# Layer 1's routing on one Trainium2 core: slots of the first token tile behind its own choice, experts of both tiles behind the slots, seven feature tiles of the rows' product at once

## The chip, the cores and the metric

The kernel runs on one core of one Trainium2 chip. The core has a matrix engine (PE in the profile; PEld is its weight load, which overlaps), a vector engine (DVE), a scalar engine (ACT), GpSimd (POOL) and SyncE (SP, which only issues transfers here), each with an instruction stream of its own that is worked off in order; they wait for each other through semaphores. Sixteen DMA engines move data between HBM and the on-chip memory. The metric is the time of one execution on the device in microseconds (us), as the median of several runs.

## The reference, cut to what matters

Two layers run over 256 latent tokens and 256 context tokens, 1024 features wide. Each layer has three mixers, a product with `w_out`, and a mixture of 16 experts, in 4 groups of 4, of which each token uses the best two of its best group. The last layer (called layer 1, counted from 0) returns latent tokens only.

```python
x_mid = x + mod_x[2] * merge_branches(px[10], y_ret, y_conv, y_mla, w_out)
h2x = rms_norm(x_mid, norm2) * (1.0 + mod_x[4]) + mod_x[3]
# moe(h2x):
scores = jax.nn.sigmoid((t @ w_router).astype(jnp.float32))
biased = scores + router_bias
grp = biased.reshape(-1, 4, 4)
group_score = jnp.sum(lax.top_k(grp, 2)[0], axis=-1)
g_sel = jnp.argmax(group_score, axis=-1)
in_grp = jnp.take_along_axis(grp, g_sel[:, None, None], axis=1)[:, 0]
idx = g_sel[:, None] * 4 + lax.top_k(in_grp, 2)[1]
w = jnp.take_along_axis(scores, idx, axis=1)
w = w / jnp.sum(w, axis=-1, keepdims=True)
for e in range(16):
    he = (jax.nn.silu(t @ w1[e]) * (t @ w3[e])) @ w2[e]
    out = out + gate[:, e:e + 1] * he
```

## The kernel before, in words

Both kernels are written as one long instruction sequence per engine. The program's own scheduler fixes those sequences before the chip starts; nothing is reordered on the chip. `with queued(ins)` and `tc.issue_after(ins)` put instructions behind a named one in that order.

The 256 latent tokens are two token tiles of 128, t=0 and t=1 (`NTT` is 2). Layer 1 comes to its experts in these steps.

- The product with `w_out` is done in two halves of 512 columns; `update` (L1138 to L1142) adds each half to the residual `resid` after a multiplication by a modulation row. The weights come as pieces of 128x1024 that are split into a high part (ACT) and a low part `wlo` (DVE, L383), and PE uses the low part last.
- `features` (L1180 to L1191) transposes `resid` and squares it, `logits_part` and `logits` (L1193 to L1206) make the 16 router scores of a tile in `lt`, `select` (L1216) the biased scores `bi`. In it `group()` finds the best group (`og`, L1240), six steps that each need the one before; `experts()` the two best experts of every group (`o1`, `o2`), eleven such steps; `finish()` keeps those of the chosen group (`sel`). In layer 1 the steps of `experts()` of t=0 run in the gaps of the next tile's work; those of t=1 are put in the list `chosen` and run during the routing.
- `norm2_rows` (L1144) makes the expert inputs `h2` (a product with a modulation row, L1147, and a second instruction, L1149) and, for t=0, its high and low part `h2h` and `h2l` (`hi_lo`, L225 and L226).
- The routing of layer 1 (L1846 to L1890): `positions` (two small matmuls, L1365 and L1366, and `posm`, L1369) numbers the tokens within their group; a comparison with a row of numbers makes the one-hot matrix `ohr` (4 instructions for each tile, L1853), whose rows are tokens and whose columns are 4 groups of 128 slots. The rows' product (L1875) multiplies `h2h` and `h2l` with it. It gathers the tokens by slots: 8 feature tiles, each four matmuls into one PSUM bank, done as two groups of four feature tiles. Each is split into `xgh` (ACT) and `xgl` (DVE) by `hi_lo`.
- `token_gates` and `gates` (L1399 to L1407, L1536 to L1538) make the weight table `gt` of tokens by experts; `slot_gates` (L1880) gathers it by slots with 16 small passes (L1885) into `gsl` (L1887).
- The 16 experts then run in order. Each has three products (`p1`, `p3`, both from `up`, and `down`), each of four weight pieces of 512 KB. For every piece ACT casts the high part `ehi` (L1093), DVE subtracts for the low part `elo` (L1095) and PE does six matmuls (L192, L193, L195). There are four buffers each for `ehi` and `elo`. `act` (L1430 to L1435) makes the activation `eth` in three instructions (tanh on ACT, two on DVE), of which the last needs the gates in `gsl`; `turn_g` transposes it (L1444) and splits it into the two parts of `gg` (L1452 and L1453), with which `down` runs. For expert 0 a function `first` holds the gate work (`slot_gates`, `act`, `turn_g`); it is called between the pieces of expert 1's `p1`, since expert 0's `down` comes after that.

Weight pieces are loaded far ahead by SP into rotating buffers (`offer`, `prefetch`); one of these, in layer 1, has the tag "mr21", which later holds a modulation row, and `fn` (the final norm's row) takes the tag of `ohr`.

## Time and profile before

| | us |
|---|---|
| median of 3 runs | 1630.13 |
| the runs | 1622.14, 1630.13, 1632.17 |
| the profiled execution | 1623.87 (span 1622.1) |
| PE busy, of the span | 1532.8 (94%) |
| DVE busy | 1161.8 (72%) |
| ACT busy | 847.0 (52%) |

The span is the time of the profiled execution from its first to its last instruction; all times of rows are counted from its start. Busy time is what an engine spent in instructions of its own. The granted clock (PEclk) is the share of PE's full speed that it was allowed in a stretch: 1.00 is 2.4 GHz, 0.50 is 1.2 GHz, and a value between is a stretch that had both.

### The profile page before, as it was taken

The numbers are of one execution on the slowest core, as the hardware profiler recorded it, in microseconds if no ns is written. First come the engines' busy times: TensorE is split into PE (matmuls) and PEld (weight loads), VectorE is DVE, ScalarE is ACT, GpSimd is POOL, SyncE is SP. The second block draws the span as 40 slices with busy tenths as digits, with TensorE's granted clock in tenths as the row PEclk, the third lists the DMA queues.
The fourth block names the chain that finished last, engine by engine and source line by source line (L and its number), as shares of the span: only waits on it lengthen the run. The fifth ranks groups of instructions, "written<-read, shape, count | busy, mean of one in ns | idle before, by whom it ended". The sixth has DMA issues, their size and how long they took to land. (4 is left out here: it accounts for less than half of the span.)

```text
span 1622.1 us, 21790 instructions
## 1 busy us (share of the span) xinstructions
PE 1532.8 (94%) x7811; PEld 1191.1 (73%) x7811; DVE 1161.8 (72%) x1978; ACT 847.0 (52%) x1218; POOL 84.8 (5%) x137
## 2 busy tenths in 40 slices
PE   4999999999999997999999969999999989999996
PEld 1766776667767884777777759888978868888775
DVE  3633376426674457899999989577676699999897
ACT  3512233334442223688788845346454467777674
POOL 1011010000000004200000210000000000000000
PEclk8999999999999998999999979999999989999998
DMA  9676354643117448999999956335436579999981
GB/s 343 190 237 227 98 169 139 192 130 105 40 53 257 164 173 300 336 376 364 377 384 373 370 172 182 104 105 150 132 90 208 180 263 371 347 390 326 361 304 64
DMA packets 238281, 370.94 MB, mean 229 GB/s; under 512 B 16147, under 2 KB 133365, under 8 KB 233045
## 3 DMA queue, kind: packets, MB, share of 16 engines
q1 hardware_dynamic: 228944, 345.06, 62.7%
q0 software_dynamic: 6400, 15.13, 3.2%
q10 hardware_dynamic: 2820, 9.28, 1.5%
q8 instruction: 64, 1.05, 0.3%
q14 instruction: 53, 0.43, 0.1%
HBM read 357.69 MB, written 11.73 MB: 228 GB/s over the span
## 5 line engine op out<-in xcount | busy, mean ns | idle before, releaser
L1095 DVE TENSOR_TENSOR elo<-eraw,ehi 128x1024 fp32r<-128x1024 f32 x291 | 344.5, 1218 | 10.3 <-ACT ehi L1093 7.9
L1093 ACT CAST ehi<-eraw 128x1024 fp32r<-128x1024 f32 x291 | 301.2, 1050 | 72.8 <-PE ps L193 44.4
L383 DVE TENSOR_TENSOR wlo<-wraw,whi 128x1024 fp32r<-128x1024 f32 (+1 forms) x146 | 176.4, 1210 | 190.0 <-ACT whi L375 187.8
L375 ACT CAST whi<-wraw 128x1024 fp32r<-128x1024 f32 (+1 forms) x146 | 151.2, 1038 | 275.3 <-PE ps L186 181.6
L185 PE MATMUL ps<-hh,whi 128*128 128x512 f32 (+1 forms) x800 | 286.8, 360 | 4.1 <-ACT hh L427 1.8
L186 PE MATMUL ps<-hl,whi 128*128 128x512 f32 (+1 forms) x800 | 276.5, 346 | 0.1
L187 PE MATMUL ps<-hh,wlo 128*128 128x512 f32 (+1 forms) x800 | 274.9, 345 | 0.3 <-DVE wlo L383 0.3
L185 PEld LDWEIGHTS ps<-hh,whi 128*128 128x128 f32 x800 | 151.1, 189 | 41.9 <-issue 16.5
L186 PEld LDWEIGHTS ps<-hl,whi 128*128 128x128 f32 x800 | 151.2, 189 | 27.8 <-issue 9.5
L187 PEld LDWEIGHTS ps<-hh,wlo 128*128 128x128 f32 x800 | 150.8, 189 | 23.3 <-issue 3.6
L192 PE MATMUL ps<-ehi,xh 128*112 128x512 f32 x256 | 104.0, 406 | 3.9 <-ACT xh L225 3.9
L193 PE MATMUL ps<-ehi,xl 128*112 128x512 f32 x256 | 103.5, 404 | 0.7 <-DVE xl L226 0.6
L192 PE MATMUL ps<-ehi,xgh 128*128 128x512 f32 x256 | 102.3, 400 | 0.2 <-ACT ehi L1093 0.2
L193 PE MATMUL ps<-ehi,xgl 128*128 128x512 f32 x256 | 101.3, 396 | 0.0
L192 PE MATMUL py<-ehi,gg 128*112 128x512 f32 (+1 forms) x240 | 93.6, 391 | 1.8 <-PEq L1562 1.6
L193 PE MATMUL py<-ehi,gg 128*112 128x512 f32 (+1 forms) x240 | 93.1, 390 | 0.0
L1095 DVE TENSOR_TENSOR elo<-raws,ehi 128x1024 fp32r<-128x1024 f32 x72 | 86.0, 1218 | 4.9 <-ACT ehi L1093 2.2
L1093 ACT CAST ehi<-raws 128x1024 fp32r<-128x1024 f32 x72 | 74.7, 1050 | 19.7 <-PE ps L193 11.0
L195 PE MATMUL ps<-elo,xgh 128*128 128x512 f32 x256 | 80.8, 396 | 1.2 <-DVE elo L1095 1.1
L195 PE MATMUL ps<-elo,xh 128*112 128x512 f32 x256 | 80.8, 397 | 0.6 <-DVE elo L1095 0.6
L195 PE MATMUL py<-elo,gg 128*112 128x512 f32 (+1 forms) x240 | 74.7, 393 | 1.5 <-DVE elo L1095 1.4
L959 ACT ACTIVATE pe<-ps,mxv 128x512 f32<-128x512 f32 (+1 forms) x48 | 29.6, 617 | 62.1 <-DVE mxv L957 58.4
(473 smaller groups left out, 2762.9 us busy)
## 6 DMA issues: line engine op xcount, KB each, us to landing
eraw<-in_w_dram SPq DMA_DIRECT2D x291, 512.0 KB
wraw<-in_w_in_dram SPq DMA_DIRECT2D x106, 512.0 KB
adaw<-in_w_ada_dram SPq DMA_DIRECT2D x40, 1024.0 KB
raws<-in_w_dram SPq DMA_DIRECT2D x72, 512.0 KB
wraw<-in_w_out_dram SPq DMA_DIRECT2D x16, 512.0 KB
wraw<-in_w_dram SPq DMA_DIRECT2D x15, 512.0 KB
yd<-ys ACTq DMA_DIRECT2D x16, 448.0 KB
eraw<-in_w_ada_dram SPq DMA_DIRECT2D x13, 512.0 KB
```

The source lines that it names most:

```text
L185: TE.matmul(ps, wp[0], xp[0], start=first, stop=False)
L186: TE.matmul(ps, wp[0], xp[1], start=False, stop=False)
L187: return TE.matmul(ps, wp[1], xp[0], start=False, stop=last).ins
L192: TE.matmul(ps, x_[0], w_[0], start=first, stop=False)
L193: TE.matmul(ps, x_[1], w_[0], start=False, stop=False)
L195: ins = TE.matmul(ps, x_[0], w_[1], start=False, stop=last)
L375: his.append(A.copy(hi[:, :kt * n], raw[:, :kt * n]).ins)
L383: return V.tensor_tensor(lo[:, :kt * n], raw[:, :kt * n], hi[:, :kt * n].bitcast(F32), op=ALU.subtract).ins
L959: A.activation(pe[:, :nk], sps[:, :nk], AF.Exp, scale=MLA_SCALE, bias=mxv[:, 1:2], accum_out=mxv[:, 2:3])
L1093: latest["hi"] = A.copy(hi, raw).ins
L1095: latest["lo"] = V.tensor_tensor(lo, raw, hi.bitcast(F32), op=ALU.subtract).ins
```

## The change

- `update` makes, for layer 1, the first product of `h2` in two halves of 512 columns, each behind its half of `resid`; `norm2_rows` leaves it out there.
- `h2h` of t=0 is cast alone; the subtraction for its `h2l` is put behind the scores `lt` of t=1.
- `positions` and the one-hot rows of t=0 (`group_slots(0)`) come directly behind the group choice of t=0. `experts` and `finish` of both tiles go into `chosen` and run behind the one-hot rows of t=1. The sum `cum` isn't made in layer 1.
- The rows' product does seven feature tiles together, in four banks of the pool `ps`, two of `py` and one of `psa`, and the eighth behind them.
- `ohr` takes the tag "mr21"; the weight buffer that had it, and later `fn`, take a new tag "fn".
- `act` names its last instruction; the reading of the overflow flag (through `latest["act"]`) and the scaling of `fn` are put behind it.

```diff
@@ def update
             V.tensor_tensor(resid[:, T, cs], resid[:, T, cs], tmp, op=ALU.add)
+            if l == 1:
+                if t not in h2:
+                    h2[t] = mg.tile([P, D], F32, name=nm("h2"), tag=("xe", "xe2")[t])
+                V.tensor_tensor(h2[t][:, cs], resid[:, T, cs], mrow[4, T // 2][:, cs], op=ALU.mult)
@@ def norm2_rows
-            V.tensor_tensor(hr, resid[:, T, :], mrow[4, T // 2], op=ALU.mult)
+            if l == 0:
+                V.tensor_tensor(hr, resid[:, T, :], mrow[4, T // 2], op=ALU.mult)
...
-                    hi_lo(h2h[:, t, :], h2l[:, t, :], hr)
+                    A.copy(h2h[:, t, :], hr)
@@ def logits
+            if l == 1 and t == 1:
+                with queued(scaled_):
+                    V.tensor_tensor(h2l[:, 0, :], h2[0], h2h[:, 0, :].bitcast(F32), op=ALU.subtract)
             select(t, lt)
@@ new
+            def group_slots(t):
...
+                rest = positions(og[:, ts, :], cumg[:, ts, :], NG, [d[:, ts, :] for d in slots_])
+                for g in range(NG):
+                    ins = V.tensor_scalar(oh[0][:, t, g, :], C("iota"), posm[:, t, g:g + 1], None, op0=ALU.is_equal)
...
@@ def select
             if l == 1:
                 run(group())
+                chosen.extend([experts, finish])
                 if t == 0:
                     V.tensor_copy(cumg[:, 1, :], og[:, 0, :])
-                else:
-                    chosen.extend([experts, finish])
-                    return
-            both = [group(), experts()] if l == 0 else [experts()]
+                    group_slots(0)
+                return
+            both = [group(), experts()]
@@ routing of layer 1
-            with queued(ins.ins):
+            ins = group_slots(1)
...
+            with queued(ins):
                 scored.append(A.copy(h2h[:, 1, :], h2[1]).ins)
                 V.tensor_tensor(h2l[:, 1, :], h2[1], h2h[:, 1, :].bitcast(F32), op=ALU.subtract)
-                run(chosen[0]())
-                chosen[1]()
+                while chosen:
+                    run(chosen.pop(0)())
+                    chosen.pop(0)()
                 for f in kept:
                     f()
                 token_gates()
...
-            for k4 in range(0, KD, 4):
-                xps = [ps_tile() for _ in range(4)]
+            xps = [ps_tile() for _ in range(4)] + [y for y, _ in ytiles()]
+            xps.append(psa.tile([P, 512], F32, name=nm("psa"), tag="psa"))
+            def rows_by_slots(ks):
...
+            rows_by_slots(range(KD - 1))
+            xps.append(ps_tile())
+            rows_by_slots([KD - 1])
@@ def act
-            V.scalar_tensor_tensor(th[:cap, :], th[:cap, :], gate, p3[:cap, :], op0=ALU.mult, op1=ALU.mult)
+            latest["act"] = V.scalar_tensor_tensor(th[:cap, :], th[:cap, :], gate, p3[:cap, :], op0=ALU.mult, op1=ALU.mult).ins
@@ expert loop
-                    fn = et("ohr", [P, D])
+                    fn = et("fn", [P, D])
...
+                    with tc.issue_after(latest["act"]):
+                        V.tensor_scalar(fn, fn, ROW_SCALE, None, op0=ALU.mult)
```

In the instruction streams the change shows at three places. The first is DVE's stream at the end of the first half of `w_out` (t is the product with the modulation row, h the expert input `h2`, wlo a weight piece's low part). Before:

```order
L1141 TENSOR_TENSOR t_2307_11617<-ps_11543,mr_11125 128x512 [waits PE_49]
L1142 TENSOR_TENSOR resid<-resid,t_2307_11617 128x512 [waits DVE_49]
L1141 TENSOR_TENSOR t_2308_11620<-ps_11544,mr_11125 128x512 [waits PE_49]
L1142 TENSOR_TENSOR resid<-resid,t_2308_11620 128x512 [waits DVE_49]
L383 TENSOR_TENSOR wlo_11631<-wraw_11629,whi_11630 128x1024 [waits DMAHW6_49,Activation_49]
L383 TENSOR_TENSOR wlo_11637<-wraw_11635,whi_11636 128x1024 [waits DMAHW7_49,Activation_49]
L383 TENSOR_TENSOR woalt_11509<-wraw_11641,woalt_11509 128x1024 [waits DMAHW0_49,Activation_49]
```

The two low parts stand directly behind the update of `resid`. And in the changed kernel:

```order
L1141 TENSOR_TENSOR t_2310_11620<-ps_11546,mr_11125 128x512 [waits PE_49]
L1142 TENSOR_TENSOR resid<-resid,t_2310_11620 128x512 [waits DVE_49]
L1141 TENSOR_TENSOR t_2312_11625<-ps_11547,mr_11125 128x512 [waits PE_49]
L1146 TENSOR_TENSOR h_2311_11623<-resid,mr_11127 128x512 [waits DVE_49]
L1142 TENSOR_TENSOR resid<-resid,t_2312_11625 128x512 [waits DVE_49]
L383 TENSOR_TENSOR wlo_11638<-wraw_11636,whi_11637 128x1024 [waits DMAHW6_49,Activation_49]
L1146 TENSOR_TENSOR h_2313_11628<-resid,mr_11127 128x512 [waits DVE_49]
L383 TENSOR_TENSOR wlo_11644<-wraw_11642,whi_11643 128x1024 [waits DMAHW7_49,Activation_49]
```

A half of h2's product now stands ahead of each of the next two low parts.

The second is DVE's stream around the gates. Here elo is a low part of a weight piece, gt the weight table, gsl the gates by slots, eth the activations of experts 0 and 1, den and w the sums and weights of `token_gates`. Before, from the fifth low part behind the rows' product to `gsl`:

```order
L1095 TENSOR_TENSOR elo_12057<-eraw_11497,ehi_12056 128x1024 [waits DMAHW1_49,PE_49,Activation_49]
L1536 TENSOR_TENSOR gt_11917<-o_2286_11533,w__2361_11858 128x2x16 [waits DVE_49]
L1537 TENSOR_TENSOR oge_11857<-o_2287_11534,w__2362_11859 128x32 [waits DVE_49]
L1095 TENSOR_TENSOR elo_12069<-eraw_11499,ehi_12068 128x1024 [waits DMAHW2_49,PE_49,Activation_49]
L1538 TENSOR_TENSOR gt_11917<-gt_11917,oge_11857 128x2x16 [waits DVE_49]
L1095 TENSOR_TENSOR elo_12082<-eraw_11501,ehi_12081 128x1024 [waits DMAHW3_49,PE_49,Activation_49]
L1543 TENSOR_TENSOR ov_12103<-og_11537,keep_11861 128x8
L1434 SCALAR_TENSOR_TENSOR eth_12113<-eth_12113,ps_11982 128x512 [waits Activation_49]
L1545 TENSOR_REDUCE cnt_12105<-ov_12103 128x1 [waits DVE_49]
L1890 TENSOR_TENSOR gov_12111<-gt_11917,ov_12103 128x32
L1095 TENSOR_TENSOR elo_12126<-eraw_11503,ehi_12125 128x1024 [waits DMAHW4_49,PE_49,Activation_49]
L1887 COPY gsl_11981<-ps_12093 128x68 [waits PE_49]
```

The changed kernel, the twelve rows up to `gsl`:

```order
L1095 TENSOR_TENSOR elo_12177<-raws_11831,ehi_12176 128x1024 [waits DMAHW1_49,PE_49,Activation_49]
L1433 RECIPROCAL den_11913<-den_11913 128x2 [waits DVE_49]
L1095 TENSOR_TENSOR elo_12188<-raws_11831,ehi_12187 128x1024 [waits DMAHW2_49,PE_49,Activation_49]
L1434 TENSOR_TENSOR w__2358_11852<-w__2358_11852,den_11913 128x2 [waits DVE_49]
L1435 TENSOR_TENSOR w__2359_11853<-w__2359_11853,den_11913 128x2
L1095 TENSOR_TENSOR elo_12199<-raws_11831,ehi_12198 128x1024 [waits DMAHW4_49,PE_49,Activation_49]
L1564 TENSOR_TENSOR gt_11918<-o_2289_11536,w__2358_11852 128x2x16 [waits DVE_49]
L1565 TENSOR_TENSOR oge_11851<-o_2290_11537,w__2359_11853 128x32 [waits DVE_49]
L1462 SCALAR_TENSOR_TENSOR eth_12255<-eth_12255,ps_12081 128x512 [waits Activation_49]
L1566 TENSOR_TENSOR gt_11918<-gt_11918,oge_11851 128x2x16 [waits DVE_49]
L1919 TENSOR_TENSOR gov_12112<-gt_11918,ov_12104 128x32 [waits DVE_49]
L1916 COPY gsl_11982<-ps_12094 128x68 [waits PE_49]
```

Low parts before carry the numbers 12057, 12069 and 12082 here and in the changed kernel 12177 to 12199: the last write of gt (L1538 before, L1566 now) moved from behind the sixth low part after the last xgl to behind the fourteenth, and behind an activation instruction of expert 1 (eth_12255).

The third is PE's stream at the same point. `ps_12080` (before) and `ps_12081` (now) are expert 1's `p1`, `gt x ohr` the gather of the gates, `cst x eth` the four transposes of expert 0's activation, `py` expert 0's `down`. Before, behind the first piece of `p1`:

```order
L195 MATMUL ps_12080<-elo_12082,xgh_11923 128x512 [waits DVE_49]
L195 MATMUL ps_12080<-elo_12082,xgh_11923 128x512
L1885 MATMUL ps_12093<-gt_11917,ohr_11863 128x17 x8
L1547 MATMUL ps_12107<-cst,cnt_12105 1x1 [waits DVE_49]
L192 MATMUL ps_12080<-ehi_12125,xgh_11923 128x512 [waits Activation_49]
L193 MATMUL ps_12080<-ehi_12125,xgl_11924 128x512
```

The gather has three more pieces of `p1` behind it. Before, around the last of these on PE:

```order
L192 MATMUL ps_12080<-ehi_12149,xgh_11923 128x512 [waits Activation_49]
L193 MATMUL ps_12080<-ehi_12149,xgl_11924 128x512
L1444 MATMUL ps_12117<-cst,eth_12113 128x128 [waits DVE_49]
L1444 MATMUL ps_12117<-cst,eth_12113 128x128 x3
L192 MATMUL ps_12080<-ehi_12149,xgh_11923 128x512
L193 MATMUL ps_12080<-ehi_12149,xgl_11924 128x512
L195 MATMUL ps_12080<-elo_12150,xgh_11923 128x512 [waits DVE_49]
L195 MATMUL ps_12080<-elo_12150,xgh_11923 128x512
L192 MATMUL py_12161<-ehi_12163,gg_12122 128x512 [waits Activation_49]
```

The transposes have four matmuls of that piece behind them, then comes `down`. The changed kernel from the last piece of `p1` on PE:

```order
L192 MATMUL ps_12081<-ehi_12150,xgh_11924 128x512
L193 MATMUL ps_12081<-ehi_12150,xgl_11925 128x512
L195 MATMUL ps_12081<-elo_12151,xgh_11924 128x512 [waits DVE_49]
L195 MATMUL ps_12081<-elo_12151,xgh_11924 128x512
L1914 MATMUL ps_12094<-gt_11918,ohr 128x17 [waits DVE_49]
L1914 MATMUL ps_12094<-gt_11918,ohr 128x17 x7
L1575 MATMUL ps_12108<-cst,cnt_12106 1x1
L1472 MATMUL ps_12118<-cst,eth_12114 128x128 [waits DVE_49]
L1472 MATMUL ps_12118<-cst,eth_12114 128x128 x3
L192 MATMUL py_12162<-ehi_12164,gg_12123 128x512 [waits Activation_49]
```

The gather of the gates and the transposes, which stood inside expert 1's `p1` with matmuls of its pieces behind them, now stand in one row behind all of `p1`, directly ahead of `down`.

## Rows read from the trace of the kernel before

**Rows 1.** Stretches: us, busy us and instructions by engine, PEclk, DMA share, GB/s.
```profile
1300.00:1320.00 20.00, 14.20 (x57) 11.40 (x58) 19.42 (x86) 11.98 (x21) 1.24 (x2) 0.74 0.79 262
1320.00:1340.00 20.00, 20.00 (x98) 16.09 (x97) 18.09 (x32) 14.16 (x16) 0.00 (x0) 1.00 0.80 275
1420.00:1520.00 100.00, 100.00 (x444) 80.71 (x443) 95.98 (x98) 76.84 (x83) 0.00 (x0) 1.00 0.98 360
```
**Rows 2.** Groups by line, 1320 to 1520: busy us, mean ns | idle before, releasers.
```profile
L1095 DVE TENSOR_TENSOR elo<-eraw,ehi 128x1024 fp32r<-128x1024 f32 x105 | 124.3, 1217 | 2.0 <-ACT ehi L1093 1.5
```
**Rows 3.** Timeline, halves of w_out: start us, us, engine line ... [idle before <-releaser].
```profile
1282.88 0.69 DVE L1142 TENSOR_TENSOR resid<-resid,t 128x512 f32<-128x512 f32 x1
...
1284.76 0.50 PE L186 MATMUL ps<-wlo,mh 128*128 128x512 f32 x1 [0.57 <-DVE wlo L383]
```
**Rows 4.** Timeline of PE from the end of w_out to the first expert.
```profile
1296.79 0.39 PE L187 MATMUL ps<-woalt,bt 128*128 128x512 f32 x1
...
1307.77 1.19 PE L1875 MATMUL ps<-ohr,h2h 128*128 128x512 f32 x2 [4.15 <-DVE gs L1235]
...
1312.72 1.09 PE L1875 MATMUL ps<-ohr,h2l 128*128 128x512 f32 x4
...
1318.11 0.40 PE L192 MATMUL ps<-ehi,xgh 128*128 128x512 f32 x1
```
**Rows 5.** Timeline of DVE from the one-hot rows of t=1 to the last xgl.
```profile
1309.51 0.88 DVE L1853 TENSOR_SCALAR ohr<-cmoe,posm 128x128 fp32r<-128x128 f32 x4
...
1314.46 0.68 DVE L226 TENSOR_TENSOR xgl<-ps,xgh 128x512 fp32r<-128x512 f32 x1
...
1319.51 0.68 DVE L226 TENSOR_TENSOR xgl<-ps,xgh 128x512 fp32r<-128x512 f32 x1
```
**Rows 6.** Timeline of DVE from the third piece's low part to the gated activation.
```profile
1320.30 1.21 DVE L1095 TENSOR_TENSOR elo<-eraw,ehi 128x1024 fp32r<-128x1024 f32 x1
1321.43 0.17 DVE L1402 TENSOR_REDUCE w__2362_11859<-oge 128x2 f32<-128x32 f32 x1
1321.53 1.21 DVE L1095 TENSOR_TENSOR elo<-eraw,ehi 128x1024 fp32r<-128x1024 f32 x1
...
1327.68 0.18 DVE L1538 TENSOR_TENSOR gt<-gt,oge 128x32 f32<-128x32 f32 x1
...
1328.99 0.67 DVE L1434 SCALAR_TENSOR_TENSOR eth<-eth,ps 128x512 f32<-128x512 f32 x1
1329.59 0.15 DVE L1545 TENSOR_REDUCE cnt<-ov 128x1 f32<-128x8 f32 x1
...
1332.60 0.23 DVE L1887 COPY gsl<-ps 128x68 f32<-128x68 f32 x1 [1.62 <-PE ps L1885]
...
1333.94 0.74 DVE L1435 SCALAR_TENSOR_TENSOR eth<-eth,gsl,ps 128x512 f32<-128x512 f32 x1
```
**Rows 7.** Timeline of PE: gather of the gates, transposes, expert 0's down.
```profile
1330.70 1.86 PE L1885 MATMUL ps<-gt,ohr 128*128 128x17 f32 x16
...
1335.97 0.60 PE L1444 MATMUL ps<-cst,eth 128*128 128x128 f32 x4
...
1337.33 0.67 PE L192 MATMUL py<-ehi,gg 128*128 128x512 f32 x2
```
**Rows 8.** Stretches around two changes of the granted clock; columns as in rows 1.
```profile
1301.00:1302.00 1.00, 0.98 (x8) 0.90 (x7) 0.94 (x7) 0.03 (x1) 0.00 (x0) 0.79 0.97 307
...
1307.80:1311.40 3.60, 3.60 (x10) 2.88 (x11) 3.53 (x11) 1.97 (x4) 0.61 (x1) 0.50 0.73 241
...
1311.00:1312.00 1.00, 1.00 (x4) 0.78 (x3) 1.00 (x5) 1.00 (x3) 0.00 (x0) 0.59 0.90 238
```
**Rows 9.** Timeline of PE: waits at the flag of layer 0 and behind expert 11.
```profile
848.50 0.49 PE L193 MATMUL ps<-ehi,xl 128*112 128x512 f32 x1 [0.63 <-DVE xl L226]
...
1538.07 0.74 PE L195 MATMUL ps<-elo,xgh 128*128 128x512 f32 x2 [0.75 <-DVE elo L1095]
...
1541.54 0.73 PE L195 MATMUL ps<-elo,xgh 128*128 128x512 f32 x2 [0.40 <-DVE elo L1095]
```

More of the change, by code (lines that the diff above doesn't have):

```diff
@@ L1182, in features @@
             cs = slice(half * 512, half * 512 + 512)
-            if half == 0:
+            if half == 0 and l == 0:
                 h2[t] = mg.tile([P, D], F32, name=nm("h2"), tag=("xe", "xe2")[t % 2])
@@ L1359, in row @@
             return C(name).unsqueeze(1).to_broadcast([P, NTT, n])
-        def positions(sel, cum, n, dst):
-            pps = ps_tile()[:, :sel.shape[1] * n]
-            TE.matmul(pps, C("ones"), cum, start=True, stop=False)
-            TE.matmul(pps, C("tri"), sel, start=False, stop=True)
-            flat = "p t e -> p (t e)"
-            posn, keep, posm = (d.rearrange(flat) for d in dst)
-            V.scalar_tensor_tensor(posm, pps, 1.0, sel.rearrange(flat), op0=ALU.add, op1=ALU.mult)
-            def rest():
-                V.scalar_tensor_tensor(keep, pps, float(cap), sel.rearrange(flat), op0=ALU.is_lt, op1=ALU.mult)
-                A.copy(posn, pps)
-            return rest
         if l == 0:
```

49 lines of the change are left out of this document (32 added, 17 removed).

## Prediction

> **What bounds the kernel now.** I read the stretches first, because the average shares of the whole span mix stages. In the expert stage (the last line of [rows 1]) PE is busy 100.00 of 100 us at the full clock, DVE 95.98 of 100: PE sets the pace and DVE follows with 4% to spare. In the routing (1300 to 1320) it is the other way round: PE works 14.20 of 20 us, and at a mean clock of 0.74, while DVE works 19.42. From 1320 to 1340 PE is full again and DVE has 18.09. So time is lost in the routing, by PE waiting for DVE's chain, and behind it every microsecond by which PE starts later or stops stays in the total, as long as nothing else is waited for. Transfers are not: over 200 us the 105 low parts of the weights stood idle for 2.0 us in all, 1.5 of them for ACT's cast and not for a piece [rows 2].
>
> Then the timeline of PE in the routing. The rows' product begins at 1307.77 after 4.15 us of nothing, and the first expert matmul at 1318.11 [rows 4]. DVE's timeline beside it: one-hot rows of t=1 at 1309.51, first `xgl` at 1314.46, eighth at 1319.51 (0.72 each with the small instructions between) [rows 5], third low part at 1320.30 and from there one low part after the other [rows 6].
>
> **The change part by part.** The program order of the changed kernel is known, so I walk it with the prices of these rows. On DVE a low part takes 1.13 until the next can begin (1320.30 to 1321.43), a small instruction 0.10 (1321.43 to 1321.53), a 128x512 activation instruction 0.60 (1328.99 to 1329.59) [rows 6].
>
> *Halves of h2's product, positions of t=0.* A half ahead of the first low part of `w_out` costs some 0.6, by the 0.69 of an instruction of its size [rows 3]; PE already waits 0.57 there for that low part, so `w_out` ends about 0.6 later, and two small passes among its last matmuls add 0.3. In return only a half instead of the whole product stands ahead of t=0's group choice, 0.6 less. I take 0 for the choice of t=0. If the cover were gone, 0.3 would be left.
>
> *`h2l` of t=0 and the one-hot rows.* `h2l` (1.13) moves from ahead of the scores of t=1 to behind them, and the biased scores of t=1 wait for it, since DVE has nothing else in its order. The four one-hot rows of t=0 (0.22 each, a quarter of the 0.88) and its slots come out of t=1's chain. I get t=1's one-hot rows some 0.6 later (1310.1 to 1310.9, bounds −0.6, if DVE used all its 0.58 idle us of 1300 to 1320, and +1.0). Small instructions that are gone from that point give 0.2 back: first `xgl` at 1314.85, eighth done at 1320.6, +0.4.
>
> *Seven feature tiles.* Both parts of t=0 now run while t=1 is still choosing. For t=1 remain 14 matmuls and the eighth tile's four, 0.23 each (four in 1.09, of which the last one's 0.40 overlaps nothing [rows 4]): from `h2l` of t=1 at about 1311 to 1315.2. The first expert matmul can start at 1315.5 instead of 1318.11, −2.6. But the third piece needs its low part, which stands behind all eight `xgl` in DVE's order: done at 1321.9, 0.4 later than before. So PE's lead is spent waiting, in bits, between 1317 and 1323.
>
> *The experts' choice behind the slots.* This is the term that decides. Before, the last write of `gt` stood behind six low parts and began at 1327.68; PE gathered the gates at 1330.70 without a wait and had matmuls of expert 1's `p1` to do until 1337.33 [rows 7], under which copy, activation and transposes lay. Now eleven steps of choosing for t=0 and eleven for t=1, `sel`, and `token_gates` are threaded between low parts, one or two to a gap. Fourteen low parts at 1.13 are 15.8, 24 small instructions 2.4, two activation instructions 1.2: 19.4 from 1320.7, so the last write of `gt` begins at 1340.1. I take off 0.2, because the many that depend on nothing recent are nearer 0.08: done at 1340.1.
> PE's `p1` of expert 1 needs the tenth of these low parts. Nine and its own 1.21, 17 small ones and one activation instruction are 13.6: 1334.3, and two more matmuls end `p1` at 1334.8. In the new order the gather is next on PE, and behind it, in order, the transposes and `down`. PE has nothing to do for 5.3 us.
> From 1340.1: gather 1.86, `gsl` and a cast 0.3, activation 0.74 (its step; 1333.94) [rows 6], transposes 0.60 and from their end 0.76 to `down` (before, 1335.97 + 0.60 to 1337.33 [rows 7]); with 0.1 to 0.2 for handing over, 1344.45. Before, `down` began at 1337.33: **+7.1**. DVE is then four pieces ahead, the most that the buffers allow, and PE is the bound to the end, so this isn't given back. From below: the fourteenth low part can't be earlier than expert 1's `p1` is done with its buffers, which leaves a gap of 3.1 whatever DVE's prices: **+5**.
>
> *The clock.* After gaps of this kind the granted clock falls: dense matmuls ended at 1297.18 [rows 4], and behind small work and pauses the stretch 1301 to 1302 shows 0.79, half way to the lower level of 1.2 GHz; 1307.8 to 1311.4, when PE had begun again, shows 0.50, and only 1311 to 1312 shows 0.59 on its way back [rows 8]. Here PE stands still for 5.3 us, so I expect the gather, and perhaps the first of `down`, at the lower level. The gather is then 1.1 to 1.9 longer, the rest 0 to 1.8: **+2.0**, bounds 0 and +3.7.
> The Trainium skill says the same against this change ("TensorE: Matmul & The Clock Gate", section "HAM oscillation — how this bites in real kernels"): a stall long enough between two bursts brings the array back to the lower clock, and the next burst starts cold. By that rule the gap costs +9.1; without it +7.1.
>
> *Two places further on.* At layer 0's flag PE waits 0.63 for an `xl` that stood behind a low part; now the low part is behind it: −0.5. Behind expert 11, PE waits 0.75 and 0.40 for low parts that stood behind the scaling of `py` [rows 9]; the new order has them ahead: −1.15, bounds 0 and −1.5.
>
> *At nothing:* buffer "fn" and the earlier loads of two rows, hidden as transfers are [rows 2] (uncovered, one piece of 512 KB is 1.5 at 360 GB/s [rows 1]); `cum`, four small instructions in a stretch already counted; the scaling of `fn`, one 0.7 us instruction on DVE with 4% to spare.
>
> **Sum.** 7.1 + 2.0 − 0.5 − 1.15 = +7.45, or +7.5 on the profiled execution's 1623.87: 1631.3. That execution lies 6 under the median of the runs shown, which spread over 10 us. The mean of these four executions is 1627.1, and I take that as the base: 1634.6, rounded to **1635**.
>
> **The rivals.**
> *The gap without the clock.* PE idles, but the clock holds: +7.1 less the 1.65 of the two places, +5.5, 1632.6. For it: from 1297.2 on PE had small work and the fall still took over 4 us, so a 5.3 us gap may just reach it.
> *The gates come in time* (the other side). One mechanism: DVE's small instructions vanish in gaps that it has anyway (1.62 idle at 1332.60 [rows 6]), and the last write of `gt` is done before `p1` of expert 1 ends. Then the earlier start counts: −2.6 − 1.65 = −4.2, 1622.9. It decides if `gt` is written 5.3 earlier than I have it, or if `p1` ends so much later; the buffers' rule (gap of 3.1) speaks against it.
> *The change doesn't do what it says.* The product is earlier, but DVE's eight `xgl` and the low parts set the same times as before, and no gap follows because I count the low parts wrongly: +0.4 − 1.65 = −1.2, 1625.9.
> *The lower clock holds into down.* PE restarts with short passes and transposes, and all four pieces of `down` run at the lower level before it returns: gap +7.1, clock +3.7, less 1.65: +9.2, 1636.3. [...]
> *Late pieces.* The standstill also holds up ACT's casts and the buffers behind them, and PE meets a second gap of its size at expert 1's own gates: +15, 1642.
>
> **Chances.** Forecast 0.43, gap without the clock 0.22, lower clock into `down` 0.10, gates in time 0.10, does nothing 0.08, late pieces 0.07. The likeliest alone: 1629 to 1640. Three runs that spread like these move a median by up to 5, so the range goes from 1624 to 1645: it leaves out the gates in time and some of the late pieces. About 1% is what a measurement of this kernel can tell, 1613.8 and 1646.4: faster 0.03, slower 0.08, within it 0.89.
>
> **What would show it.** In the changed profile: first expert matmul near 1315.5 but no gain at the third piece; an idle of 3 to 6 us in front of the gather, released by the last write of `gt` on DVE; a clock of 0.50 in the gather; `down` of expert 0 seven to eleven later. The waits at 848.50, 1538.07 and 1541.54 gone. It is wrong if the gather starts with no wait, if DVE is idle between 1321 and 1340, or if `down` starts by 1338.

## The result, and the profile after

The changed kernel takes 1639.41 us (median of 9 runs, 1636.16 to 1641.35), the kernel before 1626.52 (median of 9, 1622.14 to 1632.17): a ratio of 1.0072, 95% interval 1.0060 to 1.0084. It is slower by 0.7%. The forecast was 1635, with a range of 1624 to 1645, and "within 1%" at 0.89. The profiled execution has a span of 1639.6.

The stretches of the changed kernel, columns as in [rows 1] (us, busy us and instructions of PE, PEld, DVE, ACT, POOL, granted clock, DMA share, GB/s). They lie some 7 us later than before, because `w_out` ends at 1304.66 and no longer at 1297.18; about half of that is the scatter of executions, below.

```profile
1300.00:1320.00 20.00, 16.19 (x71) 12.86 (x70) 14.55 (x61) 7.07 (x16) 1.20 (x2) 0.74 0.62 204
1320.00:1340.00 20.00, 18.21 (x76) 13.44 (x75) 20.00 (x52) 16.15 (x22) 0.00 (x0) 1.00 0.66 220
1420.00:1520.00 100.00, 99.14 (x439) 79.72 (x438) 96.33 (x99) 75.96 (x81) 0.00 (x0) 1.00 0.94 341
```

Where [rows 1] had PE at 20.00 of 20 and DVE at 18.09, it is now DVE that has no idle time (20.00) and PE that waits for it (18.21). The timeline of PE (start, us, engine, line ... [idle before <-releaser]) shows the rest; it answers to [rows 4, 7]:

```profile
1304.26 0.40 PE L187 MATMUL ps<-woalt,bt 128*128 128x512 f32 x1
...
1319.37 1.17 PE L1900 MATMUL ps<-ohr,h2h 128*128 128x512 f32 x4 [0.60 <-DVE keep L1227]
...
1323.77 0.50 PE L192 MATMUL ps<-ehi,xgh 128*128 128x512 f32 x1
...
1330.08 0.73 PE L195 MATMUL ps<-elo,xgh 128*128 128x512 f32 x2 [1.36 <-DVE elo L1095]
...
1342.69 0.63 PE L195 MATMUL ps<-elo,xgh 128*128 128x512 f32 x2
1348.14 3.60 PE L1914 MATMUL ps<-gt,ohr 128*128 128x17 f32 x16 [4.82 <-DVE gt L1566]
1351.67 0.19 PE L1575 MATMUL ps<-cst,cnt 128*1 128x1 f32 x2
1352.85 1.11 PE L1472 MATMUL ps<-cst,eth 128*128 128x128 f32 x4 [0.99 <-DVE eth L1463]
1354.65 1.22 PE L192 MATMUL py<-ehi,gg 128*128 128x512 f32 x2 [0.69 <-ACT gg L1480]
...
1362.37 0.39 PE L192 MATMUL ps<-ehi,xgh 128*128 128x512 f32 x1
```

PE ends expert 1's `p1` at 1343.32, stands still for 4.82 us until DVE has written `gt`, gathers in 3.60 us (before, 1.86 without a wait [rows 7]), waits 0.99 for the gated activation and 0.69 for its cast, and only then begins `down`, at 1354.65. The 1.36 at 1330.08 is the third piece, whose low part stands behind all eight `xgl`. DVE at the same places, to be laid beside [rows 5, 6]:

```profile
1310.07 0.16 DVE L1224 SCALAR_TENSOR_TENSOR posm<-ps,og 128x4 f32<-128x4 f32 x1 [0.60 <-PE ps L1221]
...
1318.15 0.16 DVE L1224 SCALAR_TENSOR_TENSOR posm<-ps,og 128x4 f32<-128x4 f32 x1 [1.06 <-PE ps L1221]
...
1323.03 0.68 DVE L226 TENSOR_TENSOR xgl<-ps,xgh 128x512 fp32r<-128x512 f32 x1
...
1328.04 0.68 DVE L226 TENSOR_TENSOR xgl<-ps,xgh 128x512 fp32r<-128x512 f32 x1
...
1328.81 1.21 DVE L1095 TENSOR_TENSOR elo<-eraw,ehi 128x1024 fp32r<-128x1024 f32 x1
...
1345.97 1.21 DVE L1095 TENSOR_TENSOR elo<-raws,ehi 128x1024 fp32r<-128x1024 f32 x1
...
1347.91 0.18 DVE L1566 TENSOR_TENSOR gt<-gt,oge 128x32 f32<-128x32 f32 x1
...
1351.78 0.23 DVE L1916 COPY gsl<-ps 128x68 f32<-128x68 f32 x1 [3.47 <-PE ps L1914]
```

The low parts at 1328.81 and 1345.97 are the first and the last of the fourteen that stand between the last `xgl` and `gt`. Last, the clock (windows, columns as above): in the standstill, in the gather, and from the start of `down` to the next expert matmul.

```profile
1345.00:1346.00 1.00, 0.00 (x0) 0.00 (x0) 1.00 (x4) 0.00 (x0) 0.00 (x0) 0.73 1.05 408
1348.14:1351.74 3.60, 3.60 (x18) 3.56 (x18) 0.17 (x1) 0.00 (x0) 0.00 (x0) 0.50 1.01 377
1358.00:1359.00 1.00, 1.00 (x4) 0.80 (x3) 1.00 (x1) 0.00 (x0) 0.00 (x0) 0.50 0.00 0
1359.00:1360.00 1.00, 1.00 (x5) 0.77 (x4) 0.06 (x1) 0.70 (x1) 0.00 (x0) 0.94 0.00 0
1354.65:1362.37 7.72, 7.72 (x24) 6.08 (x25) 3.71 (x4) 3.42 (x4) 0.00 (x0) 0.71 0.24 71
```

PE's last work before the fall ends at 1343.32. The clock falls within 1345 to 1346 (0.73 on average over that microsecond), is at the lower level, 1.2 GHz, through the whole gather, and returns only at about 1359, when `down` is more than half done.

**How two executions are compared.** Executions of the same kernel differ (the kernel before took 1622.14 to 1632.17), and between its two profiles nearly all of the difference arises ahead of about 1272 us: the second (run e5_same) lies 6.77 us behind the first there, and 6.83 at the end. So I set the start of each PE matmul against the same matmul of the kernel before and read two numbers for each kernel: the *tail*, what it gains or loses from the end of layer 1's attention to the end of the span, and the *early part*, summed over the 1036 of the first 1272 us in which the kernels that move no tile repeat to 0.14 us. Times from the end of `w_out`'s last matmul:

| kernel | first expert matmul | `down` of expert 0 begins | next expert matmul | tail | early part |
|---|---|---|---|---|---|
| before | 20.93 | 40.15 | 46.03 | 0 | 0 |
| changed | 19.11 | 49.99 | 57.71 | +10.78 | +2.97 |
| e1_early | 19.19 | 40.81 | 46.68 | +3.46 | +2.90 |
| e2_late | 20.83 | 47.20 | 55.50 | +6.75 | −0.14 |
| e3_fill | 17.84 | 46.87 | 55.06 | +8.12 | +2.96 |
| e4_merged | 17.78 | 39.44 | 45.25 | +1.45 | +1.76 |
| e5_same | 20.90 | 40.13 | 46.00 | +0.06 | −0.09 |
| e6_seven | 20.41 | 40.01 | 45.90 | −0.09 | −0.02 |
| e7_lean | 18.00 | 39.68 | 45.49 | −0.80 | +1.58 |
| e9_nof | 17.74 | 48.63 | 55.90 | +8.59 | +2.8 |
| e11_aligned | 18.07 | 39.73 | 45.63 | +0.03 | +0.01 |
| e12_pool | 19.46 | 41.03 | 46.96 | +1.41 | +0.3 |

How far the tail can be trusted depends on the clock in the routing. With the routing of the kernel before, kernels repeat it to 0.1 us (e5_same +0.06, e8_alloc +0.05). The changed kernel, e3_fill and e9_nof have the same instructions in the same order up to the first expert matmul, and yet it comes at 19.11, 17.84 and 17.74. The windows of the changed kernel, then of e9_nof:
```profile
1308.00:1318.00 10.00, 8.39 (x27) 6.76 (x27) 7.97 (x30) 2.71 (x6) 1.20 (x2) 0.50 0.86 292
```
```profile
1309.60:1316.40 6.80, 4.93 (x13) 3.63 (x13) 6.28 (x29) 1.32 (x3) 0.63 (x1) 0.50 0.98 327
1316.50:1320.00 3.50, 2.81 (x14) 2.06 (x13) 3.07 (x12) 2.98 (x5) 0.57 (x1) 1.00 0.76 201
```
The lower level lasts some 10 us in one and 7 in the other. So a tail behind the changed routing carries up to 1.4 us that is a matter of the execution.

The tail of +10.78 is made up of: `w_out`'s second half +0.7; −1.8 up to the first expert matmul; +11.7 from there to `down`; +1.84 in `down` (7.72 for 5.88); +1.1 and +0.9 for two new waits further on; −2.3 behind expert 11; −1.2 near the end; −0.2 in small pieces. The +3 of the early part lies where no instruction was changed. Together 13.8; the runs measured +11.7 (9.8 to 13.7).

### The profile page after: what moved, and what is told of

Its sections match the earlier page's. It is cut to its first block, busy times and chain, and to the rows that moved or that the text cites. A ratio compares the mean times of both kernels' runs of the same rounds, so it can differ in the third digit from the quotient of the medians.

```text
span 1639.6 us, 21793 instructions
## 1 busy us (share of the span) xinstructions
PE 1545.3 (94%) x7811; PEld 1200.4 (73%) x7811; DVE 1164.4 (71%) x1979; ACT 850.1 (52%) x1218; POOL 84.5 (5%) x137
## 5 line engine op out<-in xcount | busy, mean ns | idle before, releaser
L192 PE MATMUL py<-ehi,gg 128*112 128x512 f32 (+1 forms) x240 | 95.7, 400 | 1.5 <-PEq L1590 0.9
L193 PE MATMUL py<-ehi,gg 128*112 128x512 f32 (+1 forms) x240 | 94.3, 396 | 0.0
```

What stands on the lines that cost most here:

```text
L192: TE.matmul(ps, x_[0], w_[0], start=first, stop=False)
L193: TE.matmul(ps, x_[1], w_[0], start=False, stop=False)
```

## The experiments

Each runs as a whole kernel beside the kernel before. Theory 1 of the expectations is the prediction's: the experts' choice of t=0, behind the slots, makes `gt` late, and PE's stop ahead of the gather, with the clock, is the loss. What the rivals say stands in each expectation.

**e1_early: the changed kernel with the choice of t=0 back where it was.**
```diff
-                chosen.extend([experts, finish])
                 if t == 0:
                     V.tensor_copy(cumg[:, 1, :], og[:, 0, :])
                     group_slots(0)
-                return
-            both = [group(), experts()]
+                else:
+                    chosen.extend([experts, finish])
+                    return
+            both = [group(), experts()] if l == 0 else [experts()]
...
```


> One part of the change undone: the experts of t=0 are chosen where the kernel before chose them, in the gaps of t=1's scores; everything else is the change. The last write of the gate table then stands behind seven low parts instead of fourteen, and PE's gather of the gates stands inside expert 1's p1 again. Theory 1 (the late gate table makes the loss): no wait of PE in front of the gather, expert 0's down 39 to 41 us behind the end of w_out (before 40.2, change 50.0), ratio to the kernel before 0.997 to 1.000. Theory 2 (the slots of t=0 and the seven feature tiles make the loss, by waits in the routing): down still 5 us or more later, ratio 1.004 to 1.008.


Ratio 1.0043 (1.0028 to 1.0057). PE's timeline, third piece and gather:
```profile
1328.28 0.73 PE L195 MATMUL ps<-elo,xgh 128*128 128x512 f32 x2 [1.14 <-DVE elo L1095]
...
1337.00 1.85 PE L1915 MATMUL ps<-gt,ohr 128*128 128x17 f32 x16
```
The gather waits for nothing and runs at full speed, `gt` stands behind seven low parts instead of fourteen, and `down` begins at 40.81 instead of 49.99. So the place of this choice is worth 9.2 us at `down`, as theory 1 has it. But the time should have come back to the kernel before and did not: 3.46 are left in the tail, of which 2.0 are the two new waits further on, and 2.90 in the early part.

**e2_late: the kernel before with this one edit alone.**
```diff
                 run(group())
+                chosen.extend([experts, finish])
                 if t == 0:
...
-                run(chosen[0]())
-                chosen[1]()
+                while chosen:
+                    run(chosen.pop(0)())
+                    chosen.pop(0)()
```


> One part of the change alone on the kernel before: the experts of t=0 are chosen behind the slots, with those of t=1; slots, halves and the product in two groups of four stay as before. The last write of the gate table stands behind fourteen low parts. Theory 1: PE waits 3 to 6 us in front of the gather, which runs at the lower clock; ratio to the kernel before 1.005 to 1.009. Theory 2: nothing is lost, 0.999 to 1.001.


Ratio 1.0042 (1.0029 to 1.0054), a little less than expected; tail +6.75. PE's timeline at the same place:
```profile
1344.88 2.64 PE L1884 MATMUL ps<-gt,ohr 128*128 128x17 f32 x16 [3.86 <-DVE gt L1536]
1348.63 1.11 PE L1442 MATMUL ps<-cst,eth 128*128 128x128 f32 x4 [0.99 <-DVE eth L1433]
1350.43 1.22 PE L192 MATMUL py<-ehi,gg 128*128 128x512 f32 x2 [0.69 <-ACT gg L1450]
```
The edit alone makes the standstill, the slower gather, and the waits of 0.99 and 0.69. It is the largest part of the loss, with the early part at nothing.

**e3_fill: the changed kernel with 18 more matmuls in the standstill**, whose product nobody reads.
```diff
...
+                if e == 1:
+                    spare = psa.tile([P, 512], F32, name=nm("psa"), tag="psa")
+                    with tc.issue_after(latest["mm"]):
+                        for i in range(FILL):
+                            TE.matmul(spare, xh[:, 0, :P], xh[:, i % KD, :], start=(i == 0), stop=(i == FILL - 1))
```


> The changed kernel with 18 matmuls of 128x512 more, whose result nobody uses, on PE between the end of expert 1's p1 and the gather of the gates: 4.2 us of PE work in its wait of 4.8. They take nothing from DVE. If the lower clock costs what the trace of the change shows (gather 3.60 for 1.86, expert 0's down 7.72 for 5.88, some 0.5 in the transposes, 4.1 in all), the clock stays at 1.00, the gather takes 1.9, and the loss falls from 0.72% to 0.4 to 0.5% (ratio 1.004 to 1.005). If the clock costs nothing on the path, the ratio stays at 1.007 or rises.


Ratio 1.0049 (1.0030 to 1.0069). PE's timeline:
```profile
1341.02 4.28 PE L1976 MATMUL psa<-xgh 128*128 128x512 f32 x18
1346.02 1.96 PE L1915 MATMUL ps<-gt,ohr 128*128 128x17 f32 x16 [0.72 <-DVE gt L1567]
...
1349.08 0.90 PE L1473 MATMUL ps<-cst,eth 128*128 128x128 f32 x4 [0.98 <-DVE eth L1464]
1350.66 1.22 PE L193 MATMUL py<-ehi,gg 128*128 128x512 f32 x2 [0.69 <-ACT gg L1481]
```
and the windows of the gather, of a microsecond behind it, and of `down`:
```profile
1346.02:1347.98 1.96, 1.96 (x18) 1.93 (x18) 0.17 (x1) 0.00 (x0) 0.00 (x0) 1.00 1.05 393
1349.00:1350.00 1.00, 0.90 (x4) 0.50 (x4) 0.28 (x2) 0.00 (x0) 0.00 (x0) 0.67 0.88 336
1350.66:1358.85 8.19, 8.19 (x25) 6.46 (x25) 3.71 (x4) 3.41 (x4) 0.00 (x0) 0.66 0.30 104
```
With work in the gap the gather is at the full clock: 1.96 instead of 3.60, so 1.64 of it was the clock's. But the clock did not stay up: it fell in the microsecond from 1349, after waits of 0.72 and 0.98 with only the gather's narrow matmuls between them, and `down` is no faster than without the filling (8.19, against 7.72). The clock's share in the gather is shown by this; that in `down` (+1.84, at 0.71) is read from the rows, and this run did not take it away. Of the 2.66 by which the tail is below the changed kernel's, 1.27 lie ahead of the first expert matmul, where the filling can have no part.

**e4_merged: the changed kernel with the experts of both tiles chosen by the same instructions**, on `[P, 2, 16]` instead of twice on `[P, 16]`: 14 small instructions instead of 28.
```diff
...
-                while chosen:
-                    run(chosen.pop(0)())
-                    chosen.pop(0)()
+                experts2()
```


> The changed kernel, but the experts of both token tiles are chosen by the same 14 instructions over both tiles instead of 28 over one each (the sum of the two choices, which layer 1 does not use, is left out). The last write of the gate table stands behind seven low parts. Theory 1: no wait in front of the gather, expert 0's down 38 to 41 us behind w_out, ratio to the kernel before 0.996 to 1.000. Theory 2: as the change, 1.004 to 1.008.


Ratio 1.0031 (1.0020 to 1.0042), above the expected 0.996 to 1.000; tail +1.45, in which the two new waits further on (0.89 and 0.48 here) stand as in e1_early. PE's gather and DVE's last write of `gt`, a timeline of each:
```profile
1337.80 1.85 PE L1940 MATMUL ps<-gt,ohr 128*128 128x17 f32 x16
```
```profile
1336.53 0.17 DVE L1594 TENSOR_TENSOR gt<-gt,oge 128x32 f32<-128x32 f32 x1
```
Both tiles chosen behind the slots, and yet no wait: `gt` is written 1.1 before PE wants it. What hurt was the number of small dependent instructions, each in a gap of its own between low parts, and not the place as such. `down` begins 0.71 earlier than before, in an execution with the short stretch of the lower clock (e1_early, with the long one, 0.66 later).

**e5_same: the kernel before, again**, to see what two runs of one kernel differ by.

> The kernel before once more, unchanged, as a measure of what two builds of one program differ by, and with a second profile of it. If the 3 to 5 us by which the profiled executions of all variants so far lie behind that of the kernel before at the start of w_out's second half (1272 us) are scatter of executions, this profile lies behind by as much there too, and the ratio is 0.998 to 1.002. If it lies at the same time as the first profile (within 1 us), the variants lose something ahead of the routing that the change makes.


Ratio 0.9993 (0.9981 to 1.0004).

**e6_seven: the kernel before with seven feature tiles at once**, and nothing else.
```diff
-                xps = [ps_tile() for _ in range(4)]
+            xps = [ps_tile() for _ in range(4)] + [y for y, _ in ytiles()]
+            xps.append(psa.tile([P, 512], F32, name=nm("psa"), tag="psa"))
...
```


> One part of the change alone on the kernel before: seven feature tiles of the rows' product at once, the eighth behind them; slots and the experts' choice as before. Theory (DVE sets the pace up to the third weight piece): the first expert matmul comes 1 to 2.6 us earlier behind the end of w_out than the 20.9 of before, expert 0's down less than 1 us earlier than 40.2; ratio 0.999 to 1.001. Rival (PE sets it): down 1.5 to 2.6 us earlier, ratio 0.998.


Ratio 1.0007 (0.9997 to 1.0017). The first expert matmul comes 0.5 earlier, `down` 0.14, the tail is −0.09. On its own the edit is nothing, as expected if DVE's `xgl` and low parts set the pace there and not the product.

**e10_halves: the kernel before with h2's product in halves.**
```diff
+            if l == 1:
...
+                V.tensor_tensor(h2[t][:, cs], resid[:, T, cs], mrow[4, T // 2][:, cs], op=ALU.mult)
...
```


> One part alone on the kernel before: the first product of h2 in two halves, each behind its half of resid. PE's wait for the low part in w_out grows from 0.57 to 1.05 or more, w_out ends 0.5 to 0.6 later; the group choice of t=0 comes as early as before, and behind the routing 0 to 0.6 us are lost. Ratio 0.999 to 1.001, so only the profile can tell.


Ratio 1.0000 (0.9987 to 1.0014), tail +0.06. PE's wait in `w_out`, 0.57 in [rows 3]:
```profile
1290.20 0.50 PE L186 MATMUL ps<-wlo,mh 128*128 128x512 f32 x1 [1.05 <-DVE wlo L383]
```
The 0.5 lost here come back in the routing, since half a product less stands ahead of the group choice: a change at nothing, as priced.

**e9_nof: the changed kernel without the place given to the scaling of `fn` and to the reading of the flag** (both are left where the scheduler puts them; without `latest["act"]` the reading no longer waits for an activation).
```diff
-            latest["act"] = V.scalar_tensor_tensor(th[:cap, :], th[:cap, :], gate, p3[:cap, :], op0=ALU.mult, op1=ALU.mult).ins
+            V.scalar_tensor_tensor(th[:cap, :], th[:cap, :], gate, p3[:cap, :], op0=ALU.mult, op1=ALU.mult)
...
-                    with tc.issue_after(latest["act"]):
-                        V.tensor_scalar(fn, fn, ROW_SCALE, None, op0=ALU.mult)
+                    V.tensor_scalar(fn, fn, ROW_SCALE, None, op0=ALU.mult)
```


> The changed kernel without its last part: neither the flag's reading nor the scaling of the final norm's row is put behind an activation. The wait of 0.86 us of PE for a low part at expert 4's combination should be gone, and that of 0.48 at the flag of layer 1: 1.1 and 0.9 us less by the profile from those places on, unless the waits of the kernel before at expert 12 (0.75 and 0.40) come back for them. Ratio to the kernel before 1.006 to 1.007.


What it tells apart are two waits of the changed kernel's PE. First PE's timeline, then two of DVE's, the scaling ahead of the first wait and the activation ahead of the second:
```profile
1429.43 0.73 PE L195 MATMUL py<-elo,gg 128*128 128x512 f32 x2 [0.86 <-DVE elo L1095]
...
1529.87 0.74 PE L195 MATMUL ps<-elo,xgh 128*128 128x512 f32 x2 [0.48 <-DVE elo L1095]
```
```profile
1421.66 0.69 DVE L1993 TENSOR_SCALAR fn<-fn 128x1024 f32<-128x1024 f32 x1
```
```profile
1527.93 0.75 DVE L1463 SCALAR_TENSOR_TENSOR eth<-eth,gsl,ps 128x512 f32<-128x512 f32 x1 [2.52 <-PE ps L195]
1528.60 2.35 DVE L1095 TENSOR_TENSOR elo<-eraw,ehi 128x1024 fp32r<-128x1024 f32 x2
```
At the second place two low parts stand behind an activation for which DVE waits 2.52; in e9_nof two run ahead of it and it waits 0.49. That is the flag's place and not the scaling, which ran 100 us earlier: expert 11's `p1` is put behind the reading, and the reading behind that activation. In e9_nof PE has neither wait. Its tail is +8.59, 2.2 less than the changed kernel's; but 1.4 of that lie ahead of the first expert matmul, and other stretches differ too, so the worth of the two places is read from the waits, 2.0 together. The times don't show that gain: ratio 1.0092 (1.0073 to 1.0111) from 4 runs, which is above the changed kernel's. Tail and early part add up to +11.4 us, the runs to +15.0 (11.9 to 18.1); the difference would have to lie in the stretches ahead of 1272 us that repeat in no kernel; no run shows that, and why this kernel did worse stays open.

**e8_alloc: the kernel before, with only the storage of the three slot tiles moved.** `posn`, `keep` and `posm`, 32 bytes per partition each, are reserved in the pool that lives through both layers, as the change has it. No instruction moves.
```diff
+        if l == 1:
+            slots0 = [small(tg, [P, NTT, NG], 1) for tg in ("posn", "keep", "posm")]
...
-            posn, keep, posm = slots_ = [sm(tg, NG) for tg in ("posn", "keep", "posm")]
+            posn, keep, posm = slots_ = slots0
```


> The kernel before with one thing of the change that moves no instruction: the three small slot tiles (posn, keep, posm) are reserved in the pool that lives through both layers instead of in that of the routing, which shifts the addresses of the tiles reserved behind them. Medians of the variants with this reservation lie 2 to 4 us above what their profiles show behind 1272 us; those without it don't. If addresses cost this, the ratio is 1.0015 to 1.0025; if it is scatter or something else in them, 0.999 to 1.001. Behind 1272 us no difference in either case.


Ratio 1.0033 (1.0018 to 1.0047). The tail is +0.05, the early part +3.33: the loss lies ahead of 1272 us, before layer 1 writes these tiles. The groups of one matmul line of layer 0's experts (busy us, mean ns of one), over 200 us of the kernel before, of e8_alloc and of e11_aligned (next):
```profile
L193 PE MATMUL ps<-ehi,xl 128*112 128x512 f32 x174 | 69.3, 398 | 0.6 <-DVE xl L226 0.6
```
```profile
L193 PE MATMUL ps<-ehi,xl 128*112 128x512 f32 x174 | 69.8, 401 | 0.6 <-DVE xl L226 0.6
```
```profile
L193 PE MATMUL ps<-ehi,xl 128*112 128x512 f32 x174 | 69.3, 398 | 0.6 <-DVE xl L226 0.6
```
Same instructions, same waits, and a granted clock of 1.00 in all three; in e8_alloc each is a few ns longer. It is the addresses: the 96 bytes push whatever is allocated behind them. Which operand's address it is, and what a matmul minds in it, no run here shows.

**e7_lean: e4_merged without the halves and without the places of `fn`'s scaling and of the flag's reading.**
```diff
-            if l == 1:
-                if t not in h2:
-                    h2[t] = mg.tile([P, D], F32, name=nm("h2"), tag=("xe", "xe2")[t])
-                V.tensor_tensor(h2[t][:, cs], resid[:, T, cs], mrow[4, T // 2][:, cs], op=ALU.mult)
...
-                    with tc.issue_after(latest["act"]):
-                        V.tensor_scalar(fn, fn, ROW_SCALE, None, op0=ALU.mult)
+                    V.tensor_scalar(fn, fn, ROW_SCALE, None, op0=ALU.mult)
...
```


> Experts of both tiles chosen by the same instructions, as in the run above, and two further parts of the change undone: h2's product again as one instruction behind both halves of resid, and neither the flag's reading nor the scaling of the final norm's row put behind an activation. Expected against the run with the merged choice: the 0.6 us at w_out and the 0.9 to 1.1 us behind the scaling (a wait of PE for a low part, 0.86 in the change) and 0.9 us at the flag are gone, so behind w_out about 1 us less than before; ratio to the kernel before 0.998 to 1.001. If the parts undone don't matter, it stays at 1.003.


Ratio 1.0021 (1.0009 to 1.0032): a gain was looked for, and it is a loss. The tail is −0.80, but the addresses are shifted by 288 bytes here, and the early part is +1.58.

**e11_aligned: e7_lean with its tiles laid out so that the shift is 256 bytes.**
```diff
-            posn, keep, posm = slots_ = [small(tg, [P, NTT, NG], 1) for tg in ("posn", "keep", "posm")]
+            posn, keep, posm = slots_ = [part8(i).rearrange("p (t g) -> p t g", g=NG) for i in range(3)]
...
+            V.memset(small("pad", [P, 32], 1), 0.0)
...
```


> The kernel of e7_lean with its small tiles placed so that the tiles reserved behind them move by 256 bytes a partition instead of 288: slots and maxima lie in tiles that layer 1 had no use for, and 128 bytes stay empty; the same instructions otherwise. If what costs 1.6 us (e7_lean) to 3.3 us (e8_alloc) in the steady stretches ahead of the routing is where addresses lie against some round boundary, these stretches repeat the kernel before within 0.3 us and the ratio is 0.999 to 1.001; if any shift costs this much, 1.5 to 3.5 us stay and the ratio is 1.001 to 1.003. Behind 1272 us as e7_lean, 0.5 us earlier than before.


Ratio 1.0001 (0.9989 to 1.0014): the early part is +0.01. So 96 bytes cost 3 us, 288 some 1.6 to 1.8 (e7_lean, e4_merged) and 256 nothing. The tail, however, is +0.03 and not e7_lean's −0.80. Most of that difference grows evenly through layer 1's experts, in which PE waits in neither from 1355 to 1535: e7_lean gains 0.6 there and e11_aligned loses 0.4. The addresses act there too, so e7_lean's tail was no gain of its edits.

**e12_pool: e11_aligned with `h2l` of t=0 made by GpSimd instead of DVE.**
```diff
-                with queued(scaled_):
-                    V.tensor_tensor(h2l[:, 0, :], h2[0], h2h[:, 0, :].bitcast(F32), op=ALU.subtract)
+                nc.gpsimd.tensor_tensor(h2l[:, 0, :], h2[0], h2h[:, 0, :].bitcast(F32), op=ALU.subtract)
```


> The kernel of e11_aligned, and the subtraction for h2l of t=0 on GpSimd instead of the vector engine, which has an instruction of 1.13 us less between the scores of t=1 and the first low parts. If DVE sets the pace up to the third weight piece, everything of t=1 comes 1.0 to 1.2 us earlier, PE's waits of 1.2 and 0.3 us for the first low parts shrink by as much, and behind 1272 us it is 1.3 to 1.7 us earlier than before: ratio 0.998 to 1.000. If GpSimd takes over 6 us for it or slows DVE down, PE waits for h2l instead and nothing is gained.


Ratio 1.0009 (0.9999 to 1.0019), tail +1.41: not a gain either. Nor is it shown to be a loss: 1.39 of it lie ahead of the first expert matmul, and there the clock was at 0.50 for 10 us (1304 to 1314), for 6.7 in e11_aligned. The timelines of GpSimd and of DVE:
```profile
1306.08 2.35 POOL L1207 TENSOR_TENSOR h2l<-h,h2h 128x1024 fp32r<-128x1024 f32 x1 [0.23 <-ACT cum L1226]
```
```profile
1306.07 2.37 DVE L208 SCALAR_TENSOR_TENSOR ss<-ss 128x1 f32<-128x1 f32 x1
...
1308.67 0.22 DVE L208 SCALAR_TENSOR_TENSOR ss<-ss 128x1 f32<-128x1 f32 x1
```
An instruction on one number per partition, 0.22 us a moment later, took 2.37 while GpSimd's took 2.35. DVE gained nothing by giving 1.2 us of work away, it lost 2.15 beside it. The Trainium skill says so ("SBUF — State Buffer", section "SBUF: two separate sides"): DVE and GpSimd share a pair of ports that goes to one of them for a whole instruction, and a DVE instruction with two inputs in SBUF competes for it with a GpSimd instruction that reads SBUF. The rows agree.

None of these kernels beats the one before by what can be measured. The sums of tail and early part lie inside the intervals of the measured times for all kernels but e9_nof and e7_lean (+0.8 by the sum, +3.4 measured, 1.5 to 5.2); the changed kernel, 13.8 against 9.8 to 13.7, and e4_merged, 3.2 against 3.3 to 6.8, lie at the edge.

## Why the prediction was right, and where it was not

The sign, the place and the mechanism were right, and the time lies in the range. The sum (+7.5) came to about two thirds of what the runs gave (+11.7). By its steps, with `w_out`'s 0.7 put back, so that all positions stand on the scale of the profile before:

**Halves at nothing.** Right: e10_halves.

**One-hot rows and `xgl` of t=1: +0.4.** In this execution +1.8: the first `xgl` comes 1.1 later counted from `w_out`'s end (1323.03 less 1304.66, against 1314.46 less 1297.18), and `w_out` 0.7 later. What the step did not price: the small product of `positions` now stands on PE among the rows' products, and DVE waits for it twice, 0.60 and 1.06 (L1224); in the kernel before it waits for neither. The size of the waits goes with the clock: in e9_nof, with the same instructions and the shorter stretch at 1.2 GHz, the first is gone, the second is 0.39, and the first `xgl` comes 0.3 earlier from `w_out`'s end than before (1322.25 less 1305.25), +0.4 with `w_out`'s 0.7:
```profile
1317.38 0.16 DVE L1224 SCALAR_TENSOR_TENSOR posm<-ps,og 128x4 f32<-128x4 f32 x1 [0.39 <-PE ps L1221]
...
1322.25 0.68 DVE L226 TENSOR_TENSOR xgl<-ps,xgh 128x512 fp32r<-128x512 f32 x1
```
So the +0.4 came out in one execution and not in the other. An edit that puts a small dependency on a busy engine has a price on the engine that waits, and here that price varies with the busy engine's clock.

**Seven feature tiles: −2.6 at the first expert matmul, then spent waiting.** Right in kind: −1.8 (−3.1 and −3.2 in e3_fill and e9_nof), then 1.36 and, two pieces on, 0.38 of waiting for low parts. e6_seven shows the edit worth 0.1 at `down`.

**The gap: 5.3, from below 3.1.** 4.82, released by the last write of `gt`, which stands behind fourteen low parts as walked. `gt` was 1.2 later than forecast, and the end of `p1`, the starting point of the gap, 1.7. The walk over the order of the changed kernel is what made this right; e1_early, e2_late and e4_merged confirm it from three sides. The rivals "the gates come in time" and "does nothing" fell with it, and "late pieces" too: expert 1's own transposes and `down` wait for nothing.

**The clock: +2.0, bounds 0 and 3.7.** This is the term that was too small: gather +1.74, transposes +0.5 (1.11 against 0.60 [rows 7]), `down` +1.84, together 4.1, above its upper bound (3.6 in e9_nof, where `down` takes 7.27). I had the gather at the lower level and put only "perhaps the first" of `down` there. The rival with the lower clock into `down`, which I gave 0.10, is nearest to what happened, though not all of `down` ran at the lower level; its price of +9.2 lacked the later DVE and the 2.0 of `fn` and the flag's reading. The rival "gap without the clock" fell by the 0.50 of the gather. The Trainium skill has the rule ("TensorE: Matmul & The Clock Gate", section "HAM oscillation — how this bites in real kernels"): a stall that is long enough between bursts returns the array to the lower clock, and the next burst begins cold. The 0.50 of the gather agrees. What the runs add: in e3_fill, with only 0.72 of standstill ahead of the gather, the clock held through the gather and fell behind it.

**The flag of layer 0: −0.5.** Did not happen. PE's timeline of the changed kernel has the same wait as [rows 9], 0.69 for 0.63:
```profile
852.14 0.48 PE L193 MATMUL ps<-ehi,xl 128*112 128x512 f32 x1 [0.69 <-DVE xl L226]
```
The step took from the order that a low part now stood behind `xl`; on DVE one still runs between the activation and `xl` (1.22 from 850.33, `xl` at 851.47), as before (846.70 and 847.83).

**Behind expert 11: −1.15, bounds 0 and −1.5.** The waits of 0.75 and 0.40 are gone, and one of 0.85 further on became 0.51; −2.3. Right in kind, and too small. The new order belongs to the experts' choice: e2_late, which moves nothing else, has it too and neither wait, while e1_early and e4_merged have the old order and the waits (0.75 and 0.41; 0.76 and 0.41). DVE's timeline before, with the first half of `py` scaled by itself, and in e2_late, with both in one row:
```profile
1536.19 0.69 DVE L1911 TENSOR_TENSOR eth<-py,mr 128x512 f32<-128x512 f32 x1 [1.73 <-PE py L195]
```
```profile
1551.82 1.29 DVE L1910 TENSOR_TENSOR eth<-py,mr 128x512 f32<-128x512 f32 x2 [0.72 <-PE py L195]
```
So the scheduler answers a late `gt` with another order 200 us on, and the gain goes when the standstill is cured.

**`fn` at nothing.** Wrong: +1.1. The argument was 4% to spare on DVE. But a share is a mean over 100 us; with the place given to the scaling a low part came late, and PE waited 0.86 for it. The reading of layer 1's flag behind an activation was in no term, and cost +0.9.

**What was in no step.** The addresses, +3. I read the diff for instructions and their order, and the storage of three small tiles as free.

The forecast came as near as it did in part by luck: the terms that it lacked, the addresses (+3), the longer clock (+2.1), `fn` and the flag's reading (+2.0), the later chain (+1.2) and the flag of layer 0 (+0.5), were in part answered by −1.2 near the end and −1.15 behind expert 11 that it lacked too, and the range was drawn for the spread of runs.

## What to carry to other kernels

When work is moved behind another chain, walk the new order of the engine that is full: a chain of small dependent instructions that gets one gap each between 1.2 us instructions takes as long as the long ones, and fewer, wider instructions (14 for 28 here) cure it as well as the old place does. A gap on PE costs its length and the clock behind it; here the lower level lasted through the small work that followed and into `down`. A tile that moves to another pool moves the addresses of others; a kernel that moves no instruction shows what that costs.

## What was not expected of the hardware

A matmul's duration changed with where tiles lie in SBUF, the on-chip memory: 398 ns before, 401 with the tiles behind three small ones shifted by 96 bytes per partition, 398 again at 256; over the 1036 us read, +3.33, +1.6 to +1.8 (288 bytes) and +0.01. The mechanism stays open. A 128x1 instruction of DVE took 2.37 us instead of 0.22 beside one of GpSimd. And the same instructions in the routing took 1.3 us more or less, with the lower clock (0.50) lasting 10 or 7 us.
